# Low parts of half of the FFN weights in a two-layer trunk block: added by DMA onto a negated high part instead of subtracted on VectorE

## The chip, the cores and the metric

The kernel runs on one core of one Trainium2 chip. The core has five engines that work side by side, each with its own queue of instructions in a fixed order: TensorE (PE, with its weight loads, PEld), VectorE (DVE), ScalarE (ACT), GpSimd (POOL) and SyncE (SP, which here only issues DMA loads). They wait for each other by semaphores. The metric is the device time of one execution in microseconds (us), lower is better; the median of three runs of the kernel before is 1647.92 us (1647.09 to 1648.18).

## What is computed

A trunk block of two layers over 256 latent and 256 context tokens of width 1024, in float32. Each layer has a SwiGLU FFN, a token mixer (attention beside a short convolution), and a second FFN; a last norm follows. The second FFN of layer 1 and the final output need the latent tokens only.

```python
def swiglu(h, w_i, w_o):
    g, u = jnp.split(h @ w_i, 2, axis=-1)
    return (jax.nn.silu(g) * u) @ w_o

def trunk_layer(xl, xc, ...):
    xl = xl + 0.5 * g1l * swiglu(modulate(rmsnorm(xl, norm_w[0]), sh1l, sc1l), w_ffn1_in, w_ffn1_out)
    ...
    xl = xl + g2l * mix_l
    xl = xl + 0.5 * g3l * swiglu(modulate(rmsnorm(xl, norm_w[2]), sh3l, sc3l), w_ffn2_in, w_ffn2_out)
```

`w_i` is 1024 x 5632 (g and u beside each other), `w_o` 2816 x 1024. The context runs through the same lines with the same weights, as far as it is needed.

## The kernel before

All products keep float32 precision by two parts: every operand is held as a high part, rounded to the matmul's type `fp32r`, and a low part, the rest. `mm3` (L226 to L230) makes one product of three matmuls: high weight by high x (L227), high weight by low x (L228), low weight by high x (L229).

Weights come in chunks of 128 partitions by 1024 columns (512 KB). `wload` (L208) takes a buffer of tag `wraw` (3 of them), has SP load the chunk into it (`load`, L100), and makes the parts in buffers of tags `whi` and `wlo` (5 each): `split` (L232) lets ScalarE copy the chunk into `whi` (L233) and VectorE subtract `raw - whi` into `wlo` (L234). In the mixer every fourth chunk's subtraction goes to POOL (L221). The order of instructions on each engine is set by the framework's scheduler from the program's order, its buffers and its dependences; nothing in it is written by hand but `tc.issue_after`.

An FFN goes through 22 blocks j of hidden columns, in two halves of 11:

- `gated` (L358) makes one block: it loads the chunk of g and of u, multiplies both by the normalized input `H` into PSUM tiles `mm`, and writes silu(g) times u as `hid`. In the first blocks after some norms, `AX` products (PSUM `psf`) are made ahead of the norm's factor.
- `gated_fast` (L439) makes the same for the blocks in the list `FAST` with seven instead of eight quarter products. It loads g and u, splits `wg` (the whole chunk of g) and `w22` (the second half of u, 128x512) by its own `parts`, then forms sums and differences of the raw quarters in place, and splits these as `s12` and `s34`. Its PSUM tiles are `mm` and `psg`.
- `into_x` (L320) is the product back to the width of 1024: eight output tiles m, each over n blocks (11 for an FFN half; 8 for the mixer's output), the results added into X. At the end of a stage it also drives the next `Norm`: squares `sq` on ScalarE (L279), sums `acc` on VectorE (L283), `rstd` (matmuls `psn_s`, `v` on VectorE L246, the power `r` on POOL L248, matmuls `psn_r` L251), and `apply`, which makes each 128x256 tile of the normalized input: `t` on VectorE (L301), the high part `h` on ScalarE (L302), the low part `h` on VectorE (L303).
- `ffn_end` (L527) is the last FFN: its output product is interleaved with the blocks, PSUM tiles `pse`; its output weights `wr` are scaled on VectorE first (L212).

Beside this, chunks `wa` of the modulation weights are loaded and multiplied on VectorE (`ada`, L174) during the FFNs.

Of the kernel before, what the change touches and what calls it, by code (L numbers as in the profile page):

```python
# [13 lines left out]
AF = mybir.ActivationFunctionType  # L14
ALU = mybir.AluOpType
# [5 lines left out]
NKT = D // P  # L21
# [18 lines left out]
WCH = 1024  # L40
# [15 lines left out]
LEAD = 1  # L56
EARLY_AT = (1, 1, 2, 2, 3, 3)
NT1 = 3
PACE = ((0.9, 2.15), (0.8, 1.7), (0.9, 1.75))
FAST = ((8, 10, 13, 15, 17, 19), (6, 8, 10, 12, 14, 16, 18, 20), (6, 8, 10, 12, 14, 16, 18, 20))  # L60

# [2 lines left out]
def tile_kernel(ctx: ExitStack, tc: tile.TileContext, xT, ctxT, cT, cR, w_ada, b_ada, norm_w,  # L64
                f1i, f1o, f2i, f2o, f2r, w_in, qn_w, kvn_w, w_uq, w_ukv, conv_w, w_out, fin_w,
                qtab, out):
    nc = tc.nc
# [137 lines left out]

    turn, pooled = [0], [False]

    def wload(src, n, tags=("whi", "wlo"), by=None):  # L208
        raw = slot("wraw", "wraw")[:, :n]
        load(raw, src)  # L210
        if by is not None:
            nc.vector.tensor_tensor(raw, raw, by, ALU.mult)  # L212
        w = [slot(t, "w" + p, dtype=F32R)[:, :n] for t, p in zip(tags, ("hi", "lo"))]
        turn[0] += 1
        if not (pooled[0] and turn[0] % POOLED == 0):
            split(*w, raw)
            return w
        nc.scalar.copy(w[0], raw)  # L218
        for a in range(0, n, TT):
            c = slice(a, a + TT)  # L220
            nc.gpsimd.tensor_tensor(w[1][:, c], raw[:, c], f32(w[0][:, c]), ALU.subtract)  # L221
        return w
# [9 lines left out]
    def split(hi, lo, src, eng=nc.vector):  # L232
        nc.scalar.copy(hi, src)  # L233
        return eng.tensor_tensor(lo, src, f32(hi), ALU.subtract)  # L234
# [19 lines left out]
    class Norm:  # L254
# [38 lines left out]
        def apply(self, s, R, kt):  # L293
# [5 lines left out]
            hi, lo = (h[:, cs] for h in self.H[kt])  # L299
            t1 = small.tile([P, T], F32, tag="t1", name="t1", bufs=NT1)  # L300
            nc.vector.scalar_tensor_tensor(t1, x, mod(d, 3 * i + 1, s, kt), R, ALU.mult, ALU.mult)  # L301
# [18 lines left out]
    def into_x(d, gate, streams, src, xs, nxt, pace=(0, 0)):  # L320


        n = len(xs)
        held = {}
        if nxt is not None and nxt.d < DEPTH and len(streams) == 1:
            ada_until(nxt.d, 3 * nxt.i + 1)

        def block(b):
            i = b // NKT
            if i not in held:  # L330
                held[i] = wload(src(i), WCH)
            return [v[:, b % NKT * P:(b % NKT + 1) * P] for v in held[i]]

        for ms in (range(0, NKT - SKEW), range(NKT - SKEW, NKT)):
            apart = nxt is not None and ms.stop == NKT
            if apart and nxt.d < DEPTH:
                ada_until(nxt.d, 3 * nxt.i + 1)
            for c in spans(streams, apart):
                for m in ms:
                    pt = mmtile(c)  # L340
                    for k in range(n):
                        mm3(pt, block(m * n + k), [v[:, c[0]:c[1]] for v in xs[k]], k == 0, k == n - 1)
                    for s in streams:
                        if c[0] <= s * T < c[1]:
                            xm = X[m][:, s * T:(s + 1) * T]
                            end = nc.vector.scalar_tensor_tensor(xm, pt[:, s * T - c[0]:(s + 1) * T - c[0]],  # L346
                                                                 mod(d, gate, s, m), xm, ALU.mult, ALU.add)
                            if nxt is not None:
                                nxt.add(m, s)
                                if nxt.d < DEPTH and len(streams) == 1:  # L350
                                    nxt.ahead(m, s)
                    if not apart:
                        ada(pace[1], end)
                if apart:
                    nxt.finish(c[0] // T)


    def gated(d, wi, j, nrm, streams):  # L358
# [1 line left out]
        H = nrm.H  # L360
        done = [early.pop(0) for _ in range(2)] if early else None
        if not done:
            w = [wload(wi[d, j, gu], WCH) for gu in range(2)]
        hid = pair(HID[j % HALF % 3], "hid")
        if nrm.AX and j < NAHEAD:

# [24 lines left out]
    def moving_sums(H):  # L391
# [44 lines left out]
            put(3, x)  # L436
        return out

    def gated_fast(d, wi, j, H, sums):  # L439

        g, u = (slot("wraw", "wraw") for _ in range(2))
        load(g, wi[d, j, 0])
        load(u, wi[d, j, 1])
        a, b = slice(0, TT), slice(TT, WCH)

        def parts(src):
            n = src.shape[-1]
            w = [slot(t, "w" + p, dtype=F32R)[:, :n] for t, p in (("whi", "hi"), ("wlo", "lo"))]
            split(*w, src)
            return w  # L450

        wg = parts(g)
        w22 = parts(u[:, b])
        nc.vector.tensor_tensor(g[:, a], g[:, a], u[:, a], ALU.subtract)
        nc.vector.tensor_tensor(u[:, a], u[:, a], u[:, b], ALU.add)
        nc.vector.tensor_tensor(u[:, b], u[:, b], g[:, a], ALU.subtract)
# [144 lines left out]
    def mixer(d, H, last, nxt):  # L601
# [15 lines left out]
        for c in spans([0, 1], True):  # L617
# [6 lines left out]
            product(ps, w[1], H, c)  # L624
            k1 = small.tile([P, T], F32, tag="t1", name="k1", bufs=NT1)
            k2 = small.tile([P, T], F32, tag="t1", name="k2", bufs=NT1)
            nc.vector.scalar_tensor_tensor(k1[64:96], ps[96:128], math.sqrt(QKD), qtb[96:128, cs], ALU.mult, ALU.mult)
# [145 lines left out]
        def attend(h, s, pT):  # L773
# [9 lines left out]
            r = slice(h % 2 * VD, (h % 2 + 1) * VD)  # L783
            o = small.tile([P, T], F32, tag="t1", name="o1", bufs=NT1)[r]
            nc.scalar.copy(o, ps[VD:P])
# [178 lines left out]
```

## Time and profile before

| | before |
|---|---|
| median of 3 runs | 1647.92 us |
| the profiled execution | 1648.4 us |
| its span in the profile | 1646.6 us |
| TensorE's mean granted clock | 0.997 |
| loaded by DMA | 249.72 MB, 152 GB/s on average |
| subtractions `wlo` 128x1024 on VectorE | 325, 1.227 us each |
| casts `whi` 128x1024 on ScalarE | 325, 1.050 us each |

The profile is one execution, seen by the hardware profiler. Busy time is the time in which an engine works, as a share of the span; an instruction's row gives its start and length in us, the engine, the line of the kernel, output and inputs by name, the shape, and in brackets how long its engine had been idle before it and what released it. The chain of work that ended last is followed back from the last instruction, step by step, to what it had waited for. DMA share is the mean busy share of the core's 16 DMA engines. In the FFNs a 128x512 matmul starts about 0.23 us after the one before, a 128x256 matmul 0.12 us.

### The profile page before, as it was taken

The page shows a single profiled execution, that of the slowest core. Times are in us where ns is not written, and L with a number is a line of the kernel's source. Part 1 is how long each engine was busy: PE and PEld are TensorE (multiplying, and loading weights), DVE is VectorE, ACT ScalarE, POOL GpSimd, SP SyncE. Part 2 cuts the span into 40 slices and gives each one's busy share as a digit, 9 for nine tenths or more (in the row PEclk, how much of TensorE's full clock was granted, in tenths as well). Part 3 has the DMA queues.
Part 4 walks back from the last instruction along what each step waited for, and adds up shares of the span by engine and source line. Part 5 has one row for each costly group of instructions (what it writes and reads, how often), then busy time and mean ns, then how long its engine had stood idle before and what let it go on. Part 6 is the DMA issues. An engine that isn't in the chain of part 4 may idle for free.

```text
span 1646.6 us, 24595 instructions
## 1 busy us (share of the span) xinstructions
PE 1612.0 (98%) x9677; PEld 1415.4 (86%) x9677; DVE 1248.0 (76%) x2071; ACT 688.4 (42%) x1103; POOL 57.6 (3%) x65
## 2 busy tenths in 40 slices
PE   6999999999999999999999999999999999999998
PEld 5889889889877788988998888988998998989997
DVE  5597898888477578879887879876776578776665
ACT  4434224424476443431343243431443257754443
POOL 0000000001211000000000000000000011100000
PEclk9999999999999999999999999999999999999999
DMA  9434664562222124346444533365346333345553
GB/s 374 144 114 155 223 197 162 175 205 103 72 80 71 52 103 141 122 160 211 160 140 168 192 111 116 133 233 190 128 147 219 103 99 114 128 156 190 182 190 105
DMA packets 73364, 249.72 MB, mean 152 GB/s; under 512 B 8736, under 2 KB 12960, under 8 KB 73248
## 3 DMA queue, kind: packets, MB, share of 16 engines
q1 hardware_dynamic: 72960, 247.62, 44.1%
q8 instruction: 76, 1.25, 0.3%
q10 hardware_dynamic: 288, 0.52, 0.1%
q14 instruction: 40, 0.33, 0.1%
HBM read 246.28 MB, written 1.05 MB: 150 GB/s over the span
## 4 chain that ended last, share of the span: by engine, by line
PE 95%; DVE 2%; ACT 1%; issue 1%; DMA 1%; POOL 0%; SPq 0%; POOLq 0%; DVEq 0%
PE mm L227 25%; PE mm L228 25%; PE mm L229 25%; PE psg L229 2%; PE psg L228 2%; PE psg L227 2%; PE pso L780 1%; PE pse L227 1%; PE pse L228 1%; PE pse L229 1%; PE pst L767 1%; PE mme L227 1%; PE mme L229 1%; PE mme L228 1%; PE psn_s L243 1%
## 5 line engine op out<-in xcount | busy, mean ns | idle before, releaser
L233 ACT CAST whi<-wraw 128x1024 fp32r<-128x1024 f32 (+1 forms) x349 | 354.6, 1021 | 669.1 <-PE mm L228 418.3
L234 DVE TENSOR_TENSOR wlo<-wraw,whi 128x1024 fp32r<-128x1024 f32 (+1 forms) x349 | 414.3, 1191 | 135.5 <-ACT whi L233 129.4
L228 PE MATMUL mm<-h,whi 128*128 128x256 f32 (+1 forms) x1472 | 495.9, 338 | 3.9 <-DVE h L303 3.6
L227 PE MATMUL mm<-h,whi 128*128 128x256 f32 (+1 forms) x1472 | 496.0, 341 | 1.8 <-ACT h L302 1.3
L229 PE MATMUL mm<-h,wlo 128*128 128x256 f32 (+1 forms) x1472 | 494.3, 337 | 0.0
L227 PEld LDWEIGHTS mm<-h,whi 128*128 128x128 f32 x1472 | 277.8, 190 | 38.7 <-issue 7.3
L228 PEld LDWEIGHTS mm<-h,whi 128*128 128x128 f32 x1472 | 280.0, 190 | 33.7 <-DVE h L303 5.4
L229 PEld LDWEIGHTS mm<-h,wlo 128*128 128x128 f32 x1472 | 279.8, 190 | 28.9
L228 PE MATMUL mm<-hid,whi 128*128 128x512 f32 (+1 forms) x627 | 222.5, 356 | 0.0
L229 PE MATMUL mm<-hid,wlo 128*128 128x512 f32 (+1 forms) x627 | 222.4, 356 | 0.0
L227 PE MATMUL mm<-hid,whi 128*128 128x512 f32 (+1 forms) x627 | 221.9, 356 | 0.0
L174 DVE SCALAR_TENSOR_TENSOR wa<-wa,scb 128x1024 f32<-128x1024 f32 x128 | 155.2, 1217 | 0.6
L229 PEld LDWEIGHTS mm<-hid,wlo 128*128 128x128 f32 x627 | 118.5, 189 | 16.8
L227 PEld LDWEIGHTS mm<-hid,whi 128*128 128x128 f32 x627 | 118.5, 189 | 16.7
L228 PEld LDWEIGHTS mm<-hid,whi 128*128 128x128 f32 x627 | 118.5, 189 | 16.6
L174 DVE SCALAR_TENSOR_TENSOR junk<-wa,scb 128x1024 f32<-128x1024 f32 x96 | 117.5, 1224 | 9.0 <-DMA wa<-in_w_ada 8.0
L346 DVE SCALAR_TENSOR_TENSOR X<-mm,mod,X 128x256 f32<-128x256 f32 x120 | 53.5, 478 | 51.1 <-PE mm L229 50.9
L233 ACT CAST hid<-sg 128x512 fp32r<-128x512 f32 (+1 forms) x88 | 49.1, 560 | 36.7 <-DVE sg L495 20.4
L234 DVE TENSOR_TENSOR hid<-sg,hid 128x512 fp32r<-128x512 f32 (+1 forms) x88 | 53.9, 613 | 12.2 <-ACT hid L233 12.2
L221 POOL TENSOR_TENSOR wlo<-wraw,whi 128x512 fp32r<-128x512 f32 x18 | 24.6, 1388 | 787.4 <-ACT whi L218 787.4
L227 PE MATMUL mm<-ts,whi 128*128 128x256 f32 x176 | 49.8, 283 | 0.0
L228 PE MATMUL mm<-ts,whi 128*128 128x256 f32 x176 | 49.8, 283 | 0.0
(238 smaller groups left out, 2273.4 us busy)
## 6 DMA issues: line engine op xcount, KB each, us to landing
wa<-in_w_ada SPq DMA_DIRECT2D x128, 512.0 KB, 4.4
wraw<-in_f1i SPq DMA_DIRECT2D x88, 512.0 KB, 3.6
wraw<-in_f2i SPq DMA_DIRECT2D x88, 512.0 KB, 3.5
wraw<-in_f1o SPq DMA_DIRECT2D x44, 512.0 KB, 3.5
wraw<-in_w_in SPq DMA_DIRECT2D x32, 512.0 KB, 3.5
wraw<-in_f2o SPq DMA_DIRECT2D x22, 512.0 KB, 3.5
wraw<-in_f2r SPq DMA_DIRECT2D x22, 512.0 KB, 4.2
waf<-in_w_ada SPq DMA_DIRECT2D x16, 512.0 KB, 8.2
```

The costliest lines, as they stand in the source:

```text
L174: nc.vector.scalar_tensor_tensor(junk, wt, 1.0, scb[:, s, :], ALU.mult, ALU.mult, accum_out=md[:, s, ct:ct + 1])
L221: nc.gpsimd.tensor_tensor(w[1][:, c], raw[:, c], f32(w[0][:, c]), ALU.subtract)
L227: nc.tensor.matmul(ps, w[0], x[0], start=start, stop=False)
L228: nc.tensor.matmul(ps, w[0], x[1], start=False, stop=False)
L229: last_mm[0] = nc.tensor.matmul(ps, w[1], x[0], start=False, stop=stop)
L233: nc.scalar.copy(hi, src)
L234: return eng.tensor_tensor(lo, src, f32(hi), ALU.subtract)
L243: nc.tensor.matmul(ss[:, t:t + 1], sq[:, t * P:(t + 1) * P], mean_col[n_mean], start=(i == 0), stop=(i == len(sqs) - 1))
L346: end = nc.vector.scalar_tensor_tensor(xm, pt[:, s * T - c[0]:(s + 1) * T - c[0]], mod(d, gate, s, m), xm, ALU.mult, ALU.add)
L767: end = nc.tensor.transpose(pt[:, kt * P:(kt + 1) * P], pr[:, kt * P:(kt + 1) * P], ident)
L780: end = nc.tensor.matmul(ps[r0:r0 + VD, :], V[kt][:, h * VD:(h + 1) * VD], pT[:, kt, :], start=kt < 2, stop=kt >= nkt - 2, tile_position=( ...
```

## The change

A chosen share of the FFN weights gets its low part in another way. ScalarE writes the high part as before, and then minus the raw chunk's rounded value into the buffer of the low part (a copy with scale -1, again rounded to `fp32r`). Then POOL issues a DMA that reads the same weights a second time from DRAM and adds them onto that buffer: raw minus high. VectorE's subtraction for this chunk goes away. `lent` holds the three operations. It is used for all chunks of the FFN's output product in `into_x` (not for the mixer's), for every second chunk in `gated` (in `ffn_end` too), and for `wg` and `w22` in `gated_fast`. Not touched are the mixer's weights, `wr` of the last FFN, `s12`, `s34`, and the chunks that are loaded before the first FFN.

```diff
+LENT = 2
+LEND = (1, 2, 1, 1)
...
-    def wload(src, n, tags=("whi", "wlo"), by=None):
+    def wload(src, n, tags=("whi", "wlo"), by=None, lend=0):
...
         turn[0] += 1
+        if lend and turn[0] % LENT < lend:
+            lent(w, raw, src)
+            return w
...
-                held[i] = wload(src(i), WCH)
+                held[i] = wload(src(i), WCH, lend=LEND[1] if n > NKT else 0)
...
-            w = [wload(wi[d, j, gu], WCH) for gu in range(2)]
+            w = [wload(wi[d, j, gu], WCH, lend=LEND[0]) for gu in range(2)]
...
+    def lent(w, raw, src):
+
+        nc.scalar.copy(w[0], raw)
+        nc.scalar.activation(w[1], raw, AF.Copy, scale=-1.0)
+        nc.gpsimd.dma_start(w[1], src, accum_op=ALU.add)
...
-        def parts(src):
+        def parts(src, dram=None):
...
-            split(*w, src)
+            if dram is None:
+                split(*w, src)
+            else:
+                lent(w, src, dram)
...
-        wg = parts(g)
-        w22 = parts(u[:, b])
+        wg = parts(g, wi[d, j, 0] if LEND[2] else None)
+        w22 = parts(u[:, b], wi[d, j, 1, :, b] if LEND[3] else None)
```

In the program this makes 173 such transfers: 55 for `in_f1i` of 128x1024 and 128x512 (41 and 14), 44 for `in_f1o`, 52 for `in_f2i` (44 and 8), 22 for `in_f2o`, so 151 of 512 KB and 22 of 256 KB. VectorE's subtractions of 128x1024 go from 325 to 174, those of 128x512 from 24 to 2. The matmuls are the same in number. The lines of the changed kernel are shifted: `lent` is L446 (cast `whi`), L447 (minus pass `wlo`) and L448 (DMA); `split` is L238 and L239, `apply` L306 to L308, `add`'s sum L288, `into_x`'s result L351.

The scheduler orders anew. At the start of layer 0's second FFN, where the norm's tiles are made (`mod_7` and `mod_6` are the scale and shift of this norm), VectorE has before:

```order
L301 SCALAR_TENSOR_TENSOR t_5477<-X,mod_7_131,psn_r 128x256
L301 SCALAR_TENSOR_TENSOR t_5481<-X,mod_7_131,psn_r 128x256
L301 SCALAR_TENSOR_TENSOR t_5485<-X,mod_7_131,psn_r 128x256
L346 SCALAR_TENSOR_TENSOR X<-mm,mod_5_129,X 128x256
L234 TENSOR_TENSOR wlo<-wraw,whi 128x1024
L303 SCALAR_TENSOR_TENSOR h<-t_5477,mod_6_130,h 128x256
L303 SCALAR_TENSOR_TENSOR h<-t_5481,mod_6_130,h 128x256
```

and with the change:

```order
L306 SCALAR_TENSOR_TENSOR t_5524<-X,mod_7_131,psn_r 128x256
L306 SCALAR_TENSOR_TENSOR t_5528<-X,mod_7_131,psn_r 128x256
L306 SCALAR_TENSOR_TENSOR t_5532<-X,mod_7_131,psn_r 128x256
L351 SCALAR_TENSOR_TENSOR X<-mm,mod_5_129,X 128x256
L308 SCALAR_TENSOR_TENSOR h<-t_5524,mod_6_130,h 128x256
L306 SCALAR_TENSOR_TENSOR t_5536<-X,mod_7_131,psn_r 128x256
L308 SCALAR_TENSOR_TENSOR h<-t_5528,mod_6_130,h 128x256
```

The subtraction between `t` and the first `h` is gone, and the second low part now follows a further `t`. On ScalarE at the same place, with the change, a minus pass stands between the first and the second high part `h`:

```order
L446 CAST whi<-wraw 128x1024
L307 ACTIVATE h<-t_5524,mod_6_130 128x256
L447 ACTIVATE wlo<-wraw 128x1024
L307 ACTIVATE h<-t_5528,mod_6_130 128x256
L307 ACTIVATE h<-t_5532,mod_6_130 128x256
```

Before, the three `h` follow each other there. At the boundary between the layers (`mod_1` and `mod_0` belong to the norm of layer 1's first FFN) VectorE with the change has:

```order
L308 SCALAR_TENSOR_TENSOR h<-t_8801,mod_0_133,h 128x256
L351 SCALAR_TENSOR_TENSOR X<-mm,mod_8_132,X 128x256
L306 SCALAR_TENSOR_TENSOR t_8805<-X,mod_1_134,psn_r 128x256
L306 SCALAR_TENSOR_TENSOR t_8809<-X,mod_1_134,psn_r 128x256
L306 SCALAR_TENSOR_TENSOR t_8813<-X,mod_1_134,psn_r 128x256
L288 TENSOR_TENSOR acc_5686<-acc_5686,sq 128x256
```

Before, a subtraction L234 stands behind the first of these three `t`, ahead of the last sum `acc`. In the last FFN PE has in every second block, with the change (`whi_14823` and `wlo_14824` are a lent chunk's two parts, `whi_14799` and `wlo_14800` a chunk of `wr`):

```order
L232 MATMUL mm_14830<-h_13802,whi_14823 128x256
L233 MATMUL mm_14830<-h_13802,whi_14823 128x256
L232 MATMUL pse_14063<-whi_14799,hid_14652 128x512
L233 MATMUL pse_14063<-wlo_14800,hid_14652 128x512
L234 MATMUL pse_14063<-whi_14799,hid_14652 128x512
L232 MATMUL pse_14064<-whi_14799,hid_14652 128x512
L234 MATMUL mm_14830<-h_13802,wlo_14824 128x256
```

Before, the three matmuls of a product follow each other, and the twelve of `pse` stand together behind the block. Now four of the twelve come between the lent chunk's first two matmuls and the first that uses its low part. On ScalarE two blocks of this stage read, with the change (`hid`, `sg` belong to the SwiGLU; the L446 and L447 are the lent chunk's):

```order
L447 ACTIVATE wlo_14730<-wraw_14727 128x1024
L446 CAST whi_14729<-wraw_14727 128x1024
L238 CAST whi_14736<-wraw_14734 128x1024
L389 ACTIVATE sg_14703<-mm_14653 128x256
L238 CAST whi_14799<-wraw_14796 128x1024
L238 CAST hid_14652<-sg_14703 128x256
L238 CAST whi_14817<-wraw_14815 128x1024
L446 CAST whi_14823<-wraw_14821 128x1024
L389 ACTIVATE sg_14791<-mm_14741 128x256
L447 ACTIVATE wlo_14824<-wraw_14821 128x1024
```

The minus pass stands ahead of the cast in one block, and behind it and an `sg` in the next. On POOL, which before has only the mixers' work and the powers `r` of the norms, the transfers stand in the same queue with those, here at the start of the last FFN:

```order
L239 TENSOR_TENSOR mixa<-o_13454,mixa 64x256
L448 DMA wlo<-in_f2i 128x1024 x2
L253 TENSOR_TENSOR r<-v,mhalf 128x2
L448 DMA wlo<-in_f2i 128x1024 x20
L608 TENSOR_TENSOR r<-v,mhalf 128x1 x2
```

Two transfers are issued ahead of the norm's `r` and twenty behind it.

## The prediction

> **What bounds the kernel now.** I read the page first: busy times, then the shares of the chain of work that ended last.
>
> ```profile
> span 1646.6 us, 24595 instructions
> PE 1612.0 (98%) x9677; PEld 1415.4 (86%) x9677; DVE 1248.0 (76%) x2071; ACT 688.4 (42%) x1103; POOL 57.6 (3%) x65
> PE 95%; DVE 2%; ACT 1%; issue 1%; DMA 1%; POOL 0%; SPq 0%; POOLq 0%; DVEq 0%
> ```
>
> PE works 98% of the span and carries 95% of the chain; the change leaves its 9677 matmuls as they are. What can be won is therefore PE's idle time, at most 1646.6 − 1612.0 = 34.6 us, and the start takes much of that. Second view: busy time by stretch, in stretches that lie in FFN bodies, in one that holds an FFN's start, and in the first 50 us (columns: stretch, length, busy us of PE, PEld, DVE, ACT, POOL, granted clock, DMA share, GB/s).
>
> ```profile
> 0.00:50.00 50.00, 35.70 (x308) 27.89 (x308) 24.35 (x47) 17.67 (x27) 2.91 (x8) 1.00 0.91 349
> 150.00:200.00 50.00, 50.00 (x244) 42.33 (x243) 39.05 (x62) 12.96 (x14) 0.00 (x0) 1.00 0.61 207
> 700.00:750.00 50.00, 50.00 (x270) 43.40 (x269) 37.49 (x59) 16.20 (x19) 0.00 (x0) 1.00 0.48 169
> 1550.00:1600.00 50.00, 50.00 (x354) 47.09 (x354) 32.76 (x36) 21.74 (x30) 0.00 (x0) 1.00 0.57 184
> 600.00:650.00 50.00, 49.09 (x250) 42.77 (x251) 41.17 (x75) 20.52 (x33) 0.70 (x1) 0.93 0.33 113
> ```
>
> The first 50 us lose 14.3 us while inputs arrive; no lent tile is used there. Inside the bodies PE is busy 50.00 of 50.00: no relief of VectorE can shorten them. Only the places where one stage's output is normalized for the next are left: 34.6 − 14.3 ≈ 20 us for all of them and the kernel's end together. At 600:650 PE is idle 0.91 us and its granted clock is 0.93.
>
> **The change part by part.** *Subtractions that go.* 151 lent tiles are 128x1024 and 22 are 128x512.
>
> ```profile
> L234 DVE TENSOR_TENSOR wlo<-wraw,whi 128x1024 fp32r<-128x1024 f32 x325 | 397.2, 1227 | 129.5 <-ACT whi L233 123.5 <-PE mm L229 4.3
> L234 DVE TENSOR_TENSOR wlo<-wraw,whi 128x512 fp32r<-128x512 f32 x24 | 17.1, 711 | 6.0 <-ACT whi L233 6.0
> L233 ACT CAST whi<-wraw 128x1024 fp32r<-128x1024 f32 x325 | 339.7, 1050 | 614.8 <-PE mm L228 403.2 <-PE psg L228 62.1 <-issue 59.3
> ```
>
> VectorE loses 151 × 1.227 + 22 × 0.711 ≈ 201 us. ScalarE gains a pass of the same shape as its cast: 151 × 1.050 plus 22 × about 0.62 (estimated from the 128x512 casts of hid below) ≈ 172 us, and goes from 688 to some 860 us, 52%. In the bodies both lie under PE and count nothing, as long as the low part is there in time (below).
>
> *What the subtractions delayed.* At three places a subtraction stands between an FFN's norm and PE. First, mixer 0 to the second FFN:
>
> ```profile
> 597.39 1.26 DVE L301 SCALAR_TENSOR_TENSOR t<-X,mod,psn_r 128x256 f32<-128x256 f32 x3 [0.68 <-PE psn_r L251]
> 598.96 1.22 DVE L234 TENSOR_TENSOR wlo<-wraw,whi 128x1024 fp32r<-128x1024 f32 x1
> 600.09 1.27 DVE L303 SCALAR_TENSOR_TENSOR h<-t,mod,h 128x256 fp32r<-128x256 f32 x3
> 598.46 0.51 PE L227 MATMUL mm<-h,whi 128*128 128x256 f32 x2 [0.99 <-ACT h L302]
> 600.62 0.58 PE L228 MATMUL mm<-h,whi 128*128 128x256 f32 x1 [1.66 <-DVE h L303]
> 606.13 0.41 PE L228 MATMUL mm<-h,whi 128*128 128x256 f32 x1
> 606.34 0.41 PE L229 MATMUL mm<-h,wlo 128*128 128x256 f32 x1
> 606.77 0.28 PE L228 MATMUL mm<-h,whi 128*128 128x256 f32 x1
> 606.89 0.28 PE L229 MATMUL mm<-h,wlo 128*128 128x256 f32 x1
> ```
>
> PE waits 1.66 us for the first low part h, which starts when the subtraction of 598.96 is done. In the new order that subtraction is gone: the first h comes about 1.1 us sooner. But ScalarE now has a lent tile's minus pass (1.05 us) between its first and second h, so the second comes later, and part of the 1.1 may go. After the stall a matmul starts every 0.21 us (606.13 to 606.34), from 606.77 on every 0.12 (to 606.89). From 600.62 to 606.77 that is 6.15 us at a slower pace, 6.15 × (1 − 0.12/0.21) ≈ 2.6 us lost, which is where the granted clock of 0.93 comes from. If the shorter idle keeps the clock up, they come back. Term: −3 us, bounds −0.5 (half a stall's 1.1, clock as before) and −3.7 (all of 1.1 and 2.6).
>
> Second, the boundary between the layers:
>
> ```profile
> 962.72 1.22 DVE L234 TENSOR_TENSOR wlo<-wraw,whi 128x1024 fp32r<-128x1024 f32 x1
> 964.64 0.41 DVE L283 TENSOR_TENSOR acc<-acc,sq 128x256 f32<-128x256 f32 x1
> 965.11 0.61 PE L243 MATMUL psn_s<-mean,acc 128*128 128x1 f32 x4 [1.21 <-DVE acc L283]
> ```
>
> PE waits 1.21 us for the sum acc, which stands behind t and that subtraction. Without it acc comes up to 1.1 us sooner; ScalarE's pass may again push a little. Term −0.9, bounds 0 and −1.2. Third, the start of the last FFN:
>
> ```profile
> 1457.31 1.22 DVE L234 TENSOR_TENSOR wlo<-wraw,whi 128x1024 fp32r<-128x1024 f32 x1
> 1459.31 0.39 PE L228 MATMUL mm<-h,whi 128*128 128x256 f32 x1 [0.37 <-DVE h L303]
> 1461.99 0.36 PE L227 MATMUL mm<-h,whi 128*128 128x256 f32 x1 [0.51 <-DVE f L374]
> 1465.37 0.50 PE L227 MATMUL pse<-whi,hid 128*128 128x512 f32 x1 [1.71 <-ACT hid L233]
> ```
>
> Three waits, 0.37 + 0.51 + 1.71 = 2.59 us. The first goes, since the subtraction ahead of h is no longer there; the second and third hang on VectorE's queue and then ScalarE's hid, whose engine is now fuller. Half is my value: term −1.3, bounds 0 and −2.6. The two boundaries into the mixers keep their order and count 0.
>
> *The new wait.* The low part of a lent tile now comes from cast, minus pass, and a transfer that POOL issues. No row shows such a transfer; call the time from its issue to its landing X. The nearest rows:
>
> ```profile
> wraw<-in_f2i SPq DMA_DIRECT2D x88, 512.0 KB, 3.5
> wkraw<-in_w_ukv SPq DMA_DIRECT2D x2, 256.0 KB, 2.8
> waf<-in_w_ada SPq DMA_DIRECT2D x16, 512.0 KB, 8.2
> DMA to landing us min/median/max: 3.4/3.9/4.5
> 593.60 0.70 POOL L248 TENSOR_TENSOR r<-v,mhalf 128x2 f32<-128x2 f32 x1 [23.42 <-DVE v L246]
> ```
>
> The fourth line is for the loads of 1500:1600. From below: a plain load 3.5 plus a small POOL operation's 0.7, 4.2. From 256 to 512 KB the time grows by 0.7 us; if adding moves every byte twice, 3.5 + 2 × 0.7 + 0.7 ≈ 5.6. From above: two loads one after the other and the POOL operation, 7.7 at 3.5 each; in the crowded start a single load took 8.2, and that is the upper end. I take 6, the doubled load and a little for queueing, since it builds on rows of these very weights.
>
> The Trainium skill, "Collectives: The Full Stack", section "The bandwidth ceiling: the fold count and why AG ≠ RS ≠ AR", says that an add in the DMA path reads two sources for each write and reaches about half the rate of a copy (32.35 against 62.28 GB/s). No row here shows an add; by that rule the sum stays as it is, for the doubled load is already what I take, but queueing weighs more: in 1550:1600 its 22 lent tiles would cost double share.
>
> How long may X be? The tightest tiles, in the last FFN and right behind the seven-product tiles of the other FFNs:
>
> ```profile
> 1535.11 1.05 ACT L233 CAST whi<-wraw 128x1024 fp32r<-128x1024 f32 x1 [1.75 <-PE mm L228]
> 1536.07 0.38 ACT L384 ACTIVATE sg<-mm 128x256 f32<-128x256 f32 x1
> 1543.73 0.28 PE L229 MATMUL mm<-h,wlo 128*128 128x256 f32 x1
> 700.54 0.40 PE L227 MATMUL mm<-h,whi 128*128 128x512 f32 x1
> 700.77 0.40 PE L228 MATMUL mm<-h,whi 128*128 128x512 f32 x1
> 691.92 1.05 ACT L233 CAST whi<-wraw 128x1024 fp32r<-128x1024 f32 x1 [1.30 <-PE mm L228]
> 693.13 0.62 ACT L233 CAST hid<-sg 128x512 fp32r<-128x512 f32 x1 [0.15 <-DVE sg L385]
> 701.01 0.39 PE L229 MATMUL mm<-h,wlo 128*128 128x512 f32 x1
> ```
>
> The cast started at 1535.11 ends at 1536.16 and the low part is first used at 1543.73: 7.57 us, of which the minus pass takes 1.05 and, in half of these tiles, sg another 0.38 ahead of it. X may be 6.1 to 6.5 by the old order. In the new order PE takes four 128x512 matmuls ahead of that first use in every second such tile, and in the others the minus pass stands ahead of the cast. Four at 0.23 us (starts 700.54 and 700.77) are 0.9, so X may be 6.9 to 7.5. At 691.92 it is 701.01 − 692.97 = 8.04, less 1.05: about 7. Of the 173 lent tiles 22 stand like the first and some 11 like the second; about 35 more have 10 to 12 us, the rest more. So at X = 6 nothing waits: term 0. X = 7.5 costs up to 0.4 us at about 15 tiles, 6 us. X = 8 costs about 0.9 us at 11 and half a microsecond at 18 others, some 19 us. X = 8.2, the upper end, costs about 25.
>
> *Traffic.* The second reading adds 151 × 0.524 + 22 × 0.262 ≈ 85 MB. In the last FFN (rows above, 184 GB/s at a share of 0.57) 22 tiles in some 170 us add 68 GB/s, a share of 0.21, or 0.42 if each byte counts twice: 0.78 to 0.99. Loads there are fetched ahead, so they hide until that share fills; near 1 it costs through X, and is in its range. POOL's power operation for the norm (0.70 us) stands behind lent issues, but those are some microseconds old by then: 0, at worst one issue, 0.7 us, at three boundaries.
>
> **Sum.** The profiled execution took 1648.4 us, its span plus 1.8 around it. −3 − 0.9 − 1.3 = −5.2 gives 1643.2; against the median of the runs (1647.92, 0.5 lower) 1642.7. I give 1643.2.
>
> **The rivals.** *Slower: PE waits for the added low part.* Decides from X ≈ 7. For it: nothing hides a late low part, PE has no slack in the bodies, and the last FFN's loads already take up to 4.5 us. Against: the doubled load gives 5.6. Price at X = 8: +19 − 5.2 gives about 1662; at the upper end 1648.4 + 25 − 5.2 ≈ 1668; were one added transfer to take 9 us, every tight tile would lose 1.5 us, 33 × 1.5 ≈ 50, and 1693. Chance 0.32.
>
> *No change: the boundaries stay as long as they are.* ScalarE's minus pass takes the subtraction's place in the norm's chain, the clock drops as before, and only parts of the 1.1 us are won: −1 to −2, about 1647. A mechanism of its own with the same result: each transfer is held by one VectorE subtraction (1.22 us, above), so X = 7.2, and with the tightest tiles 0.2 us late, 20 × 0.2 = 4 us eat what is won: 1647 as well, a chance of 0.05 within this case's. Chance 0.18 in all. The Trainium skill, "SBUF — State Buffer", section "SBUF: two separate sides", warns of just this: descriptors of a POOL-issued DMA can't be written while VectorE runs an operation that takes both ports; nothing in this trace shows it. That the change doesn't do what it says, the scheduler putting the new transfers so late that they set their own bound, would look like the first rival.
>
> *ScalarE binds*, since it gets 172 us more: at 52% it stays far below VectorE's old 76%, so it binds only where hid waits behind one more pass; twice 1.05 at the third boundary's 1465.37 would be +2, inside the second rival.
>
> **How the numbers follow.** Forecast, low parts in time and boundaries shortened: 0.50, 1640.5 to 1645. No change 0.18, slower 0.32. About 0.2%, 3.3 us, is what a measurement of this kernel can tell from no change. The forecast's 1643.2 is 4.7 below the median, so most of it counts as faster; what of it ends above 1644.6 goes to no change: 0.49, 0.19 and 0.32. For 8 in 10 the range goes from 1639 to 1668: all three largest gains give 1648.4 − 3.7 − 1.2 − 2.6 = 1640.9, less 0.5 for the median and as much again for the runs' spread (1647.09 to 1648.18) and small gains elsewhere; above stands X at its upper end.
>
> **What would show it.** Right: PE busy 50.00 in every body stretch, no wait of PE released by a POOL-issued transfer, X below 7, VectorE near 1047 us and ScalarE near 860, the PE wait at the second FFN's start below 1 us and its clock near 1.00, acc's wait at the layers' boundary near 0. Wrong: stalls ahead of matmuls that use a lent low part in the last FFN at steps of 8.5 us, or X beyond 7.5; then the slower rival holds. If VectorE falls by 201 us and the boundaries are as before, the second does.

## The result, and the profile after

The changed kernel takes 1719.56 us (median of 4 runs, 1718.49 to 1720.39) against 1647.51 us before on the same chip: 72 us more, a ratio of 1.0437 with a 95% interval of 1.0419 to 1.0455. The forecast was 1643.2 us, its range ended at 1668. The profiled execution took 1718.49 us. Its page, first the busy times and the chain of work that ended last:

```profile
span 1716.7 us, 25075 instructions
PE 1631.9 (95%) x9677; PEld 1424.7 (83%) x9677; DVE 1073.1 (63%) x1898; ACT 838.0 (49%) x1276; POOL 209.6 (12%) x238
PE 59%; issue 18%; DMA 13%; DVE 4%; ACT 3%; POOL 2%; SPq 0%; POOLq 0%; DVEq 0%; ACTq 0%
```

VectorE fell by 175 us and ScalarE rose by 150, somewhat less than the 201 and 172 counted. But PE now works 95% of its span, not 98%, and DMA has 13% of the chain where it had 1%. The span is 70.1 us longer. PE's busy time alone rose by 19.9 us, from 1612.0 to 1631.9, though the matmuls are the same, so some of them run slower (the mean granted clock is 0.988 here and was 0.997 before). The other 50 us are idle time of PE, and the waits that end with the landing of an added low part make up 37 of them. The DMA queues and the issues on the same page (packets, MB, share of the 16 engines; then median us from issue to landing) say why:

```profile
q1 hardware_dynamic: 72960, 247.62, 42.1%
q0 software_dynamic: 24912, 84.95, 26.5%
...
wa<-in_w_ada SPq DMA_DIRECT2D x128, 512.0 KB, 6.7
wraw<-in_f1i SPq DMA_DIRECT2D x88, 512.0 KB, 4.9
wraw<-in_f2i SPq DMA_DIRECT2D x88, 512.0 KB, 4.4
wraw<-in_f1o SPq DMA_DIRECT2D x44, 512.0 KB, 8.0
wlo<-in_f1o POOLq DMA_DIRECT2D x44, 512.0 KB, 9.0
wlo<-in_f2i POOLq DMA_DIRECT2D x44, 512.0 KB, 8.2
wlo<-in_f1i POOLq DMA_DIRECT2D x41, 512.0 KB, 8.1
```

The rows of before for two kinds of plain load:

```profile
wa<-in_w_ada SPq DMA_DIRECT2D x128, 512.0 KB, 4.4
wraw<-in_f1o SPq DMA_DIRECT2D x44, 512.0 KB, 3.5
```

The adding queue q0 moves a third as many bytes as SP's queue q1 and keeps the engines busy for 26.5% against 42.1%: per MB 0.312% against 0.170%, 1.8 times as long. X, the time from issue to landing that the forecast took as 6 us, is 8.1 to 9.0 in the middle. And the plain loads got slower as well, those of `in_f1o` from 3.5 to 8.0 us, those of the modulation weights `wa` from 4.4 to 6.7. The stretches that answer to those shown of before:

```profile
150.00:200.00 50.00, 50.00 (x248) 42.53 (x247) 21.73 (x39) 23.01 (x25) 9.56 (x11) 1.00 1.03 282
200.00:250.00 50.00, 45.59 (x225) 38.41 (x225) 40.08 (x71) 12.78 (x15) 3.48 (x4) 1.00 0.79 233
1100.00:1150.00 50.00, 46.07 (x234) 39.21 (x234) 20.44 (x38) 23.13 (x27) 6.95 (x8) 0.93 0.92 251
1600.00:1650.00 50.00, 45.73 (x305) 41.78 (x305) 21.90 (x26) 23.16 (x30) 4.30 (x5) 0.97 0.82 217
```

In 150:200, where the share was 0.61, it is 1.03: full (each packet counts in the stretch in which it starts, so the share can pass 1). PE loses about 4 us in 200:250 and in 1100:1150, and as much in 1600:1650, in the last FFN. There the wait is plain to see (timeline of one lent chunk of the last FFN: start, length, engine and line, idle time before it and what ended it):

```profile
1611.69 1.05 ACT L446 CAST whi<-wraw 128x1024 fp32r<-128x1024 f32 x1 [1.61 <-PE mm L233]
...
1612.92 1.05 ACT L447 ACTIVATE wlo<-wraw 128x1024 fp32r<-128x1024 f32 x1
1614.37 0.86 POOL L448 DMA_DIRECT2D wlo<-in_f2i  x1 [13.56 <-ACT wlo L447]
1623.17 0.39 PE L234 MATMUL mm<-h,wlo 128*128 128x256 f32 x1 [1.77 <-DMA wlo<-in_f2i]
```

Between POOL's issue at 1614.37 and the first matmul with this low part lie 8.8 us; PE stood idle for the last 1.77.

All kernels below have the same 9677 matmuls, so the start of the k-th matmul tells where time is gained and lost. The table gives this start before, and how much later (+) or earlier (−) it is in the full change and in four experiments:

| k-th matmul, and place | before, us | full change | e1 | e3 | e4 | e5 |
|---|---|---|---|---|---|---|
| 1200, layer 0, first FFN, second half | 220.9 | +0.9 | −0.5 | +1.7 | +1.2 | +2.0 |
| 1800, same FFN, later | 321.6 | +14.3 | −0.9 | +6.2 | +7.9 | +6.1 |
| 2700, in mixer 0 | 485.7 | +22.4 | −0.5 | +12.4 | +8.3 | +6.5 |
| 3300, at mixer 0's end | 593.6 | +22.4 | −0.5 | +12.4 | +8.3 | +6.5 |
| 3600, in layer 0's second FFN | 653.9 | +20.4 | −4.1 | +11.2 | +4.8 | +3.0 |
| 5100, at its end | 922.5 | +30.5 | −4.1 | +13.4 | +7.7 | +6.4 |
| 5700, in layer 1's first FFN | 1027.8 | +37.2 | −5.3 | +20.1 | +6.5 | +5.2 |
| 6600, same FFN, second half | 1187.8 | +43.9 | −5.9 | +28.1 | +9.2 | +9.6 |
| 8100, in mixer 1 | 1417.9 | +45.3 | −5.3 | +28.1 | +9.3 | +10.2 |
| 8700, in the last FFN | 1499.1 | +53.4 | −7.3 | +28.1 | +14.6 | +19.0 |
| 9600, near its end | 1626.4 | +69.5 | −7.3 | +28.1 | +32.8 | +34.4 |

With the full change 45 us are lost before the last FFN, 8 at its start, 16 in its body. Only between rows 3300 and 3600, at the start of layer 0's second FFN, is something gained, 2.0 us.

### The profile page after: what moved, and what is told of

Read it like the earlier page. It is cut to its first block, busy times and chain, and to the rows that moved or that the text cites. A ratio compares the mean times of both kernels' runs of the same rounds, so it can differ in the third digit from the quotient of the medians.

```text
span 1716.7 us, 25075 instructions
## 1 busy us (share of the span) xinstructions
PE 1631.9 (95%) x9677; PEld 1424.7 (83%) x9677; DVE 1073.1 (63%) x1898; ACT 838.0 (49%) x1276; POOL 209.6 (12%) x238
## 3 DMA queue, kind: packets, MB, share of 16 engines
q1 hardware_dynamic: 72960, 247.62, 42.1%
q0 software_dynamic: 24912, 84.95, 26.5%
HBM read 331.21 MB, written 1.05 MB: 194 GB/s over the span
## 4 chain that ended last, share of the span: by engine, by line
PE 59%; issue 18%; DMA 13%; DVE 4%; ACT 3%; POOL 2%; SPq 0%; POOLq 0%; DVEq 0%; ACTq 0%
PE mm L234 15%; PE mm L232 15%; PE mm L233 15%; DMA wlo<-in_f2i 5%; DMA wa<-in_w_ada 3%; POOL wlo L448 2%; DMA wraw<-in_f1o 2%; DMA wlo<-in_f1i 1%; PE pso L794 1%; PE psg L233 1%; PE psg L234 1%; PE psg L232 1%; PE pst L781 1%; DVE junk L176 1%; DVE wa L176 1%
## 5 line engine op out<-in xcount | busy, mean ns | idle before, releaser
L234 PE MATMUL mm<-h,wlo 128*128 128x256 f32 (+1 forms) x1472 | 497.4, 340 | 23.1 <-DMA wlo<-in_f2i 19.9
L234 PEld LDWEIGHTS mm<-h,wlo 128*128 128x128 f32 x1472 | 280.7, 191 | 59.9 <-DMA wlo<-in_f2i 25.8
L238 ACT CAST whi<-wraw 128x1024 fp32r<-128x1024 f32 x176 | 183.1, 1044 | 283.9 <-PE mm L233 98.9
L446 ACT CAST whi<-wraw 128x1024 fp32r<-128x1024 f32 (+1 forms) x173 | 172.1, 995 | 276.0 <-PE mm L233 112.9
L239 DVE TENSOR_TENSOR wlo<-wraw,whi 128x1024 fp32r<-128x1024 f32 x176 | 216.2, 1230 | 71.3 <-ACT whi L238 65.9
L234 PE MATMUL mm<-hid,wlo 128*128 128x512 f32 (+1 forms) x627 | 226.1, 361 | 9.7 <-DMA wlo<-in_f2o 6.4
L232 PE MATMUL mm<-hid,whi 128*128 128x512 f32 (+1 forms) x627 | 225.2, 360 | 3.6 <-ACT hid L238 3.6
L233 PE MATMUL mm<-hid,whi 128*128 128x512 f32 (+1 forms) x627 | 225.8, 360 | 0.0
L447 ACT ACTIVATE wlo<-wraw 128x1024 fp32r<-128x1024 f32 (+1 forms) x173 | 172.8, 999 | 4.6 <-PE pse L233 4.6
L234 PEld LDWEIGHTS mm<-hid,wlo 128*128 128x128 f32 x627 | 120.7, 193 | 27.5 <-DMA wlo<-in_f2o 6.6
L232 PEld LDWEIGHTS mm<-hid,whi 128*128 128x128 f32 x627 | 120.6, 192 | 21.1 <-ACT hid L238 4.4
L233 PEld LDWEIGHTS mm<-hid,whi 128*128 128x128 f32 x627 | 120.6, 192 | 17.0
L448 POOL DMA_DIRECT2D wlo<-in_f1i x55 | 48.1, 875 | 440.8 <-ACT wlo L447 350.6
L448 POOL DMA_DIRECT2D wlo<-in_f2i x52 | 45.5, 875 | 420.4 <-ACT wlo L447 273.1
L239 DVE TENSOR_TENSOR hid<-sg,hid 128x512 fp32r<-128x512 f32 (+1 forms) x88 | 54.1, 614 | 51.5 <-ACT hid L238 51.5
L351 DVE SCALAR_TENSOR_TENSOR X<-mm,mod,X 128x256 f32<-128x256 f32 x120 | 53.5, 479 | 46.7 <-PE mm L234 46.5
```

The source lines that it names most:

```text
L232: nc.tensor.matmul(ps, w[0], x[0], start=start, stop=False)
L233: nc.tensor.matmul(ps, w[0], x[1], start=False, stop=False)
L234: last_mm[0] = nc.tensor.matmul(ps, w[1], x[0], start=False, stop=stop)
L447: nc.scalar.activation(w[1], raw, AF.Copy, scale=-1.0)
L448: nc.gpsimd.dma_start(w[1], src, accum_op=ALU.add)
```

## The experiments

Two theories stood against each other. **A, latency**: one transfer takes too long by itself, and PE waits only at the tight chunks that the forecast named. **B, traffic**: adds and loads fill the DMA engines together, so that adds are stretched and plain loads come late too. Each kernel is the changed one with a small edit, unless it says otherwise. Ratios are to the kernel before, run on the same chip.

### e1: no transfer

```diff
-        nc.gpsimd.dma_start(w[1], src, accum_op=ALU.add)
```

> Leaves out the adding transfer: the low part of a lent chunk stays minus the rounded chunk, so only ScalarE's extra pass and VectorE's missing subtraction remain. If the whole loss comes from the transfers (late low parts, crowded DMA engines), it is gone and the boundary gains of the forecast show: 1640 to 1646 us, PE 50.00 of 50 in all FFN bodies, DMA share as before. If ScalarE's 172 us or the new order of instructions cost time, it stays above 1655 us.

Measured: 1641.06 us against 1647.35, ratio 0.9967 (0.9955 to 0.998). The page:

```profile
PE 1608.5 (98%) x9677; PEld 1412.6 (86%) x9677; DVE 1075.3 (66%) x1898; ACT 838.8 (51%) x1276; POOL 57.6 (4%) x65
```

Without the transfers the whole loss is gone, with ScalarE's extra passes and VectorE's relief in place. The table shows the gains where the forecast had put them: −3.6 us between 3300 and 3600, −1.2 between 5100 and 5700, −2.0 between 8100 and 8700. So the transfers, and nothing else in the change, cost some 78 us.

### e2: a copy instead of an add

```diff
-        nc.gpsimd.dma_start(w[1], src, accum_op=ALU.add)
+        nc.gpsimd.dma_start(w[1], src)
```

> The same transfers from POOL, but as a plain copy of the weights over the low part instead of an add (the low part is then the raw chunk). If the adding itself is what fills the DMA engines (84.95 MB take 26.5% of them, against 42.1% for 247.62 MB of plain loads: 1.8 times as much per byte), the queue's share falls to about 15%, a transfer takes 5 to 6 us from issue to landing instead of 8.5, and the time falls to 1650 to 1665 us. If a transfer issued by POOL is slow whatever it does, it stays near 8 us and the time above 1695.

Measured: 1652.14 us, ratio 1.0029 (1.0018 to 1.0041). The queue and three issues:

```profile
q0 software_dynamic: 24912, 84.95, 15.1%
...
wlo<-in_f1o POOLq DMA_DIRECT2D x44, 512.0 KB, 6.1
wlo<-in_f2i POOLq DMA_DIRECT2D x44, 512.0 KB, 6.0
wlo<-in_f1i POOLq DMA_DIRECT2D x41, 512.0 KB, 5.6
```

The same bytes in the same packets from the same engine take 15.1% of the DMA engines instead of 26.5%, and X is 6 us instead of 8 to 9. Of the 78 us 67 hang on the adding. How long one transfer of 512 KB takes with next to nothing beside it, first the add (full change, at 1692.3), then the copy (this run, at 1624.8), from the view of POOL's issuing line:

```profile
L448 POOL DMA_DIRECT2D wlo<-in_f2i x1: 862/862/862, 1692.3 to 1692.3; - x1
DMA to landing us min/median/max: 5.4/5.4/5.4
```

```profile
L448 POOL DMA_DIRECT2D wlo<-in_f2i x1: 530/530/530, 1624.8 to 1624.8; - x1
DMA to landing us min/median/max: 3.6/3.6/3.6
```

Alone an add takes 5.4 us and a copy 3.6; POOL needs 0.86 us to issue the one and 0.53 the other. With 256 KB an add alone takes 4.0 us (e10 below, at 1624.8) and a copy 2.9 (this run, at 655.7). So the second half of the bytes costs a copy 0.7 us and an add 1.4, twice that, as the forecast had reckoned. Alone, X = 5.4 is under the forecast's 6.

### e3: only the output products

```diff
-LEND = (1, 2, 1, 1)
+LEND = (0, 2, 0, 0)
```

> Only the chunks of the output products are lent (66 transfers of 512 KB), all of which have at least 13 us from cast to first use of the low part. Theory A (a transfer is too long by itself, 5.4 us when alone, and only tight tiles wait): no loss, 1645 to 1648 us. Theory B (adds and the modulation and weight loads together fill the DMA engines, transfers stretch to 9 us and the loads come late too): DMA share in 150:200 near 0.9 and a loss of 5 to 25 us at 200:260, 390:410 and the two other ends of output products, 1652 to 1672 us.

Measured: 1676.01 us, +28.7, ratio 1.0175 (1.0145 to 1.0204), beyond the 5 to 25 us that B expected and far from A's zero. The table puts 8.0 us of it between 5700 and 6600, in the first half of layer 1's first FFN. That stretch, and what loaded there (view of SP's issuing line in 1100:1140, in this run and then before):

```profile
1100.00:1150.00 50.00, 44.91 (x196) 36.70 (x195) 14.97 (x28) 18.14 (x20) 7.84 (x9) 0.93 1.01 288
...
DMA to landing us min/median/max: 4.3/12.0/17.3
```

```profile
DMA to landing us min/median/max: 3.3/4.7/5.3
```

The DMA engines are full (1.01), a plain load takes 12.0 us in the middle and 17.3 at most, where it took 4.7 and 5.3. What PE waits for stands at the end of chains that begin with a late load (timeline, two places):

```profile
1117.69 1.04 ACT L446 CAST whi<-wraw 128x1024 fp32r<-128x1024 f32 x1 [8.65 <-DMA wraw<-in_f1o]
1120.25 0.80 PE L232 MATMUL mm<-hid,whi 128*128 128x512 f32 x1 [3.93 <-ACT hid L238]
1121.27 0.63 PE L234 MATMUL mm<-hid,wlo 128*128 128x512 f32 x1
1121.69 0.63 PE L232 MATMUL mm<-hid,whi 128*128 128x512 f32 x1
...
946.36 1.22 DVE L176 SCALAR_TENSOR_TENSOR junk<-wa,scb 128x1024 f32<-128x1024 f32 x1 [4.03 <-DMA wa<-in_w_ada]
952.18 0.81 ACT L284 ACTIVATE sq<-X 128x256 f32<-128x256 f32 x2 [8.40 <-DVE X L351]
952.90 1.04 ACT L446 CAST whi<-wraw 128x1024 fp32r<-128x1024 f32 x1
963.19 0.58 PE L234 MATMUL mm<-hid,wlo 128*128 128x256 f32 x1 [4.27 <-DMA wlo<-in_f2o]
```

At 1117.69 ScalarE has waited 8.65 us for a plain load of an output weight; `hid`, which PE needs, stands behind that cast in ScalarE's queue, and PE waits 3.93 us, not for an add at all. Behind that wait a matmul starts every 0.42 us (1121.27 to 1121.69) instead of every 0.23: a wait costs more than its own length. In the whole run PE's busy time is 8.5 us above before.

At 963.19 PE waits 4.27 us for an add, but that add took only 7.9 us. Its cast came late, at 952.90, because in ScalarE's queue it stood behind squares that waited 8.40 us for VectorE's `X`, and VectorE's queue stood behind a modulation load (4.03 us idle ahead of 946.36). Four other waits for an add, of about 1 us each, are at chunks whose low part PE wanted 7.4 to 7.5 us after the pass, so the 13 us that were expected for every chunk were not there. All five make 8.4 us. Theory A can't give the rest of the 28.7.

### e4: only the ordinary blocks

```diff
-LEND = (1, 2, 1, 1)
+LEND = (1, 0, 0, 0)
```

> Only every second chunk of the ordinary blocks is lent (77 transfers of 512 KB, 22 of them in the last FFN). Theory A: the last FFN loses about 17 us as with the full change, the rest nothing, 1660 to 1666 us. Theory B: the last FFN's share is as full as with the full change (0.75 to 0.82), so the same 17 us there, and up to 10 more in the other FFNs: 1663 to 1677 us.

Measured: 1679.05 us (1676.68 and 1681.42), +31.7, ratio 1.0193 (1.0159 to 1.0228): 13 us over A's range and 2 over B's. The adds are 63, not the 77 of the expectation. The last FFN's body loses 18.2 us by the table (+14.6 to +32.8), as both expected; its start loses 5.3 more, and 9.3 are lost before it, with the gains at the boundaries already taken off. PE's waits for adds before the last FFN are seven and sum to 8.8 us. These adds took 8.0 to 9.3 us, each at a chunk whose low part PE wanted 7.4 to 7.7 us after the pass: the forecast's second kind of tight chunk. So here PE waits for adds at tight chunks alone, as A has it; what A lacks is that the add takes 8 to 9 us and not 5.4.

### e5: less traffic from the modulation weights

```diff
-        load(wt, w_ada[d, m, ct])
+        c = slice(0, 256)
+        load(wt[:, c], w_ada[d, m, ct][:, c])
...
-            nc.vector.scalar_tensor_tensor(junk, wt, 1.0, scb[:, s, :], ALU.mult, ALU.mult,
+            nc.vector.scalar_tensor_tensor(junk[:, c], wt[:, c], 1.0, scb[:, s, c], ALU.mult, ALU.mult,
```

> The full change, but of each modulation chunk only 256 of 1024 columns are loaded and multiplied (the modulation values are then those of a quarter of the sum): 50 MB less of plain loads, mostly in the first FFNs and beside the output products. Theory B (crowded DMA engines): the losses beside the output products and at 200:260 shrink, transfers there fall from 9 us towards 7, and of the 72 us 25 to 40 go, 1680 to 1695 us, while the last FFN, which loads none of these, keeps its 17. Theory A (each transfer is too long by itself): the loss stays, 1708 to 1720 us.

Measured: 1684.36 us, so 35 us less than the full change, within B's range. By the table 35.1 of the 45.3 us lost before the last FFN are gone, and between 5700 and 6600 the loss falls from 6.7 to 4.4 us. From 8100 to 9600, in the last FFN and its start, it is 24.2 us in both. Half of the whole loss thus needs the modulation loads beside the adds. The edit also takes time off VectorE (905 us busy instead of 1073); what of the 35 us is due to that wasn't separated. The adds themselves took 8.0 to 8.5 us here, hardly less: what shrank is the lateness of loads and of what queues behind them.

### e6: every fourth block chunk

```diff
-LENT = 2
-LEND = (1, 2, 1, 1)
+LENT = 4
+LEND = (1, 0, 0, 0)
```

> Like e4_only_gated, but every fourth chunk of the ordinary blocks instead of every second (LENT 4): in the last FFN half as many adds on the DMA engines. If the average share of the DMA engines sets the time of a transfer, it falls there from 8.4 us to about 6.5 and the last FFN loses under 3 us. If each transfer is stretched by the loads that are issued at the same moment (the raw buffer comes free when ScalarE's pass ends, and SP's next load starts with the add), it stays at 7.5 to 8.5 us and the last FFN loses about half of 18, 7 to 10 us.

Measured: 1669.94 us, ratio 1.0134 (1.0115 to 1.0152). POOL's adds in 1520:1690 took 8.0 us in the middle, against 8.3 in e4, with half as many of them:

```profile
DMA to landing us min/median/max: 5.5/8.0/9.3
```

So in the last FFN it isn't the number of adds that stretches one from 5.4 to 8 us. What fits is that each add meets a load: in an ordinary block and an output product ScalarE's pass is the raw buffer's last reader, so SP's next load of 512 KB starts when the add does, as here in e3:

```profile
1118.64 1.05 ACT L447 ACTIVATE wlo<-wraw 128x1024 fp32r<-128x1024 f32 x1
1119.71 0.33 SPq L102 DMA_DIRECT2D wraw<-in_f1o  x1
1120.09 0.86 POOL L448 DMA_DIRECT2D wlo<-in_f1o  x1 [10.30 <-ACT wlo L447]
```

The pass ends at 1119.69, the load is issued at 1119.71, the add at 1120.09. A kernel that holds the two apart wasn't tried; e9 below comes near it. The last FFN lost 4.1 us at its start and 11.8 in its body, more than the 7 to 10 expected. And with half the adds PE is idle in the body no less than in e4, by the stretch of the body in e4 and here:

```profile
1513.50:1659.20 145.70, 134.37 (x903) 123.83 (x902) 65.18 (x76) 71.21 (x93) 13.05 (x15) 0.96 0.78 212
1509.50:1648.60 139.10, 128.23 (x901) 119.35 (x901) 74.89 (x86) 66.21 (x88) 6.96 (x8) 1.00 0.69 195
```

PE's idle time is 11.3 and 10.9 us (11.5 in the full change). The losses, 18.2 and 11.8 (16.1 in the full change), differ by the pace of the matmuls: the granted clock is 0.96 and 1.00 (0.99 in the full change). So fewer late adds did not mean less waiting, since nearly each of those left was late; what sets the clock after such waits stays open.

### e10 and e11: fewer bytes in each add

e4 with the add cut to 512, and to 128, of 1024 columns.

```diff
+        n = raw.shape[-1] // 2
-        nc.gpsimd.dma_start(w[1], src, accum_op=ALU.add)
+        nc.gpsimd.dma_start(w[1][:, :n], src[:, :n], accum_op=ALU.add)
```

> Like e4_only_gated, but each transfer adds only the first 512 of the 1024 columns (the other half of the low part stays minus the rounded chunk): 256 KB instead of 512. If the time of a transfer beside loads goes by its bytes, it falls from 8.4 us to about 6, the last FFN loses under 3 us of its 18 and the time is 1646 to 1653 us. If an add has a long fixed time whatever its size, it stays above 7.2 us and the time above 1660.

> The same with 128 of 1024 columns, 64 KB: by bytes a transfer takes 3.5 to 4.5 us and no matmul waits, 1642 to 1646 us, as low as the chunks that are lent here can bring it. With a long fixed time it stays above 6.5 us, and the last FFN still loses a few us.

Measured: 1650.73 us (ratio 1.0021, 1.0009 to 1.0032) and 1644.19 us (0.9985, 0.9973 to 0.9997). The three sizes in the same places, from the issues of e4, e10 and e11:

```profile
wlo<-in_f2i POOLq DMA_DIRECT2D x36, 512.0 KB, 8.3
```

```profile
wlo<-in_f2i POOLq DMA_DIRECT2D x36, 256.0 KB, 6.2
```

```profile
wlo<-in_f2i POOLq DMA_DIRECT2D x36, 64.0 KB, 4.6
```

It is close to a straight line: 4.6 to 6.2 is 1.6 us for 192 KB, 6.2 to 8.3 is 2.1 for 256 KB, both 8.2 to 8.3 us for each 1000 KB, on about 4.1 us that are there at all three sizes. Bytes explain half of X beside loads, a fixed part the other half. The last add of each kernel, which runs alone, took 2.7 us for 64 KB (e11), 4.0 for 256 (e10) and 5.7 for 512 (e4): loads beside an add cost it 1.9, 2.2 and 2.6 us. At 64 KB the gains at the boundaries stand alone in the profiled execution, the fastest of its kernel, as in e1; the median is 3 us above e1's.

### e9: only the seven-product blocks

```diff
-LEND = (1, 2, 1, 1)
+LEND = (0, 0, 1, 1)
```

> Only the chunks of the seven-product blocks are lent (22 adds of 512 KB and 22 of 256 KB). If the three parts add up to the 72 us, this one costs 72 - 28.7 - 31.7, about 12 us, 1659 us. If the whole is more than its parts because all of them crowd the same DMA engines, it costs under 6 us: its first products come 6 to 8 us after the pass, and the time is 1645 to 1654 us.

Measured: 1649.05 us, +1.3, ratio 1.0009 (0.9998 to 1.0021). Its 512 KB adds took 5.9 and 7.0 us in the middle (those of `in_f2i` and of `in_f1i`) and hurt little. In these blocks the raw quarters are read again behind ScalarE's pass, for the sums, so the next load into that buffer doesn't start with the add. In the trace 13 of the 22 adds of 512 KB had at most one load still under way 1.5 us after their issue, and 10 of these 13 landed in 5.5 to 6.0 us, nearly as if alone; of the nine with more loads beside them eight took 7.2 to 9.5 us. That bears out e6's account. The three parts alone cost 28.7 + 31.7 + 1.3 = 61.7 us; the other 10 of the 72 come only when all run together.

### e7 and e8: only where VectorE's relief is worth something

e7 lends only in the first three ordinary blocks of the two FFNs that follow another stage's norm. e8 is the kernel before, with one chunk's subtraction of each of those blocks on GpSimd, in two halves, as the mixers do it.

```diff
-LEND = (1, 2, 1, 1)
+LEND = (1, 0, 0, 0)
...
-            w = [wload(wi[d, j, gu], WCH, lend=LEND[0]) for gu in range(2)]
+            w = [wload(wi[d, j, gu], WCH, lend=LEND[0] if j < 3 and len(streams) == 2 else 0) for gu in range(2)]
```

```diff
-    def wload(src, n, tags=("whi", "wlo"), by=None):
+    def wload(src, n, tags=("whi", "wlo"), by=None, aside=False):
...
-        if not (pooled[0] and turn[0] % POOLED == 0):
+        if not (aside or pooled[0] and turn[0] % POOLED == 0):
...
-            w = [wload(wi[d, j, gu], WCH) for gu in range(2)]
+            w = [wload(wi[d, j, gu], WCH, aside=gu == (j < 2) and j < 3 and len(streams) == 2) for gu in range(2)]
```

> Lends only four to five chunks: every second one of the first three ordinary blocks of layer 0's second FFN and layer 1's first FFN, those whose subtraction stood in the norm's way in the forecast's first two places. If those places gain as in e1_no_transfer (-3.5 and -1.3 us) and the few transfers, near quiet DMA engines, are in time: 1641.5 to 1643.5 us. If a late transfer of one of them stalls PE, 1645 to 1650 us.

> The kernel before, with no transfer and no extra pass on ScalarE: the subtraction of three chunks at each of the same two places goes to GpSimd in two halves (1.39 us each in the mixers). If what counts is only that VectorE is free there: -3.5 and -1.3 us, 1641.5 to 1643.5 us. If the norm's power operation on GpSimd waits behind the halves, up to 2.8 us of it is given back, 1645 to 1648 us.

Measured: e7 1644.89 us, ratio 0.9982 (0.9973 to 0.9991), and e8 1647.4 us, 0.9998 (0.9989 to 1.0007); e8's profiled execution is its slowest, 1651.09 us. Six adds of 512 KB (four to five were expected), of 7.5 to 8.3 us each, bring 3 us, between the two ranges expected, and e7 beats both kernels, if by no more than a measurement can just tell. By matmul starts it gains 2.2 us at the start of layer 0's second FFN and 3.5 with the layers' boundary. e8 shows that taking the subtraction off VectorE isn't enough if GpSimd does it (e8, VectorE and POOL at the first place, then at the layers' boundary):

```profile
595.65 2.72 POOL L221 TENSOR_TENSOR wlo<-wraw,whi 128x512 fp32r<-128x512 f32 x2 [0.96 <-ACT whi L218]
595.92 1.31 DVE L283 TENSOR_TENSOR acc<-acc,sq 128x256 f32<-128x256 f32 x1 [0.79 <-ACT sq L279]
598.52 2.70 POOL L221 TENSOR_TENSOR wlo<-wraw,whi 128x512 fp32r<-128x512 f32 x2 [0.16 <-ACT whi L218]
599.42 2.48 DVE L303 SCALAR_TENSOR_TENSOR h<-t,mod,h 128x256 fp32r<-128x256 f32 x3
...
954.53 0.16 DVE L246 TENSOR_SCALAR v<-psn_s 128x2 f32<-128x2 f32 x1
955.53 0.70 POOL L248 TENSOR_TENSOR r<-v,mhalf 128x2 f32<-128x2 f32 x1
```

The three `h` took 1.27 us before and take 2.48 beside GpSimd's subtraction; `acc` took 0.42 and takes 1.31. At the first place the power operation `r` wasn't late, so the expected wait is not what ate the gain there. At the boundary it was: `v` ended at 954.69, and `r` started 0.8 us later, right behind two halves.

## Why the prediction was wrong, point by point

**The bound, and the gains at the boundaries: right.** Term by term from e1, where nothing covers them: −3.6, −1.2 and −2.0 against −3, −0.9 and −1.3. In e1 the first place's 1.66 us wait for the low part `h` is gone, the wait ahead of it grew from 0.99 to 1.43, and the granted clock in 590:620 is 1.00 instead of 0.89, as argued (before, then e1):

```profile
590.00:620.00 30.00, 27.06 (x179) 25.31 (x179) 19.71 (x45) 13.38 (x26) 1.39 (x2) 0.89 0.15 53
590.00:620.00 30.00, 28.10 (x197) 25.70 (x196) 19.55 (x47) 18.97 (x33) 1.40 (x2) 1.00 0.19 56
```

In e7, with the same order and the same waits of PE at this place, the clock fell to 0.94 and only 2.2 us were won; why it fell there isn't settled.

**ScalarE's extra passes: right.** They cost nothing that can be seen (e1), with ScalarE busy 838 us where 860 were forecast.

**X: mis-sized.** The working by bytes, 5.6 us, holds for an add that runs alone (5.4), and so does its step of twice 0.7 us from 256 to 512 KB (1.4). The step that failed is the next one, "the doubled load and a little for queueing", 6 us: beside loads an add took 8.1 to 9.0 in the middle, not 6, and the queueing is not 0.4 us but 3. A load stands beside the add, because both are released by the same pass (e6); the traces of e9 bear out that this is the main reason, but no experiment changed it alone. The slower rival's price for this was about right as far as waits go: it had 19 us at X = 8 and 25 at X = 8.2, and in the full change, with X at 8.4 in the last FFN, PE's waits for adds at the ordinary chunks sum to 27 us, 19 of them in the last FFN and 8 before it.

**Traffic: the step that cost most.** The forecast worked out the DMA share for the last FFN only and said that loads "hide until that share fills". It left out 150:200, whose row it had quoted with a share of 0.61, and where every output chunk is lent. There and at the like place of layer 1 the share went to 1.03 and 0.92, loads of 3.5 us took 8.0, modulation loads 6.7, and casts and VectorE's products waited behind them in their queues. Of the 45 us lost before the last FFN, 8 are the ordinary chunks' waits above, X's part. For the other 37 no term of the sum stood, and the range's upper end, made of X alone, could not hold them. They are waits of 10 us for adds onto output chunks, waits for ScalarE and VectorE behind late loads, and slower matmuls. e5 fits: with less modulation traffic 35 of the 45 go, and the 10 that stay are about what e4, which lends no output chunk, loses there, 9.3. Most of this could be reckoned from rows at hand: 66 output chunks of 512 KB at twice the plain price, the doubling that the forecast used elsewhere, beside a share of 0.61.

**The pace after a wait: left out of the price.** The forecast counted 2.6 us of slow matmuls behind the 1.66 us wait at its first place, as something to win. For the slower rival it priced each wait at its own length alone. In the full change 20 of the 70 us are matmuls that take longer. How much a wait costs so isn't fixed: about 11 us of idle time cost 11.8 to 18.2 us in the last FFN's body.

**The Trainium skill's rule**, "Collectives: The Full Stack", section "The bandwidth ceiling: the fold count and why AG ≠ RS ≠ AR", of about half the rate for an add, stated there for the ring of a collective: the trace of this kernel agrees, with 0.312% against 0.170% of the engines for each MB (1.8 times). The forecast drew only the price of one transfer from it, and said that queueing would weigh more without pricing it. The rule of the Trainium skill, "SBUF — State Buffer", section "SBUF: two separate sides", on VectorE holding off POOL's descriptors: no run here shows it. POOL's issue of an add took 0.86 to 1.05 us in the whole of the full change, 0.87 in the middle, so it was never lengthened by as much as one VectorE subtraction, 1.22 us.

## What to carry to other kernels

Work off VectorE's queue is worth what the waits behind it are worth: here 175 us of it bought some 6 us (e1), nearly all at the three places where a norm feeds PE. Before a stage is given more DMA, work out the share of the DMA engines in each stage, the fullest first, with the new traffic at its own price per byte: once a stage is full, the transfers already there come late too, and here half of the loss needed them (e5). A transfer's time alone is not its time in a kernel that streams weights: 5.4 us became 8 to 9. And a wait of PE can cost more than its own length, when the matmuls behind it run slower.

## What the runs showed that was not expected

An add of 512 KB takes 5.4 us alone and a copy by the same queue 3.6; beside loads an add takes about 4.1 us plus 8.2 us for each 1000 KB (e4, e10, e11). Plain loads beside adds can take longer than the adds: 12.0 us in the middle and 17.3 at most at a share of 1.01 (e3). And VectorE's operations run at half speed or less beside GpSimd's subtraction of 128x512 tiles: 2.48 us for three that take 1.27, 1.31 for one that takes 0.42 (e8).
